# Attention stage of a two-layer trunk: queries' low part on GpSimd, scales in PSUM, two key tiles rounded by ScalarE

## The chip, the cores and the metric

The kernel is one program on one core of a Trainium2 chip. The metric is the device time of one execution in microseconds (us); for the kernel before, it is the median of three runs. A core has five engines that run side by side and wait for each other through semaphores: TensorE (PE, with its weight loads shown apart as PEld), VectorE (DVE), ScalarE (ACT), GpSimd (POOL) and SyncE (SP), which issues most DMAs. Each works through its own instructions in order.

## The reference, cut to what matters

The kernel computes a trunk of two layers, a state-space mixer and then attention, each followed by a feed-forward block, for 1024 latent tokens and 256 context tokens. The change lies in the attention of the second layer. There, queries and keys have 96 features in each of 16 heads, values have 64, and every latent query reads all 1280 keys:

```python
MLA_H = 16
MLA_QK = MLA_NOPE + MLA_ROPE        # 96

def softmax_attend(q, k, v):
    s = jnp.einsum('bqhd,bkhd->bhqk', q, k).astype(jnp.float32) * (MLA_QK ** -0.5)
    p = jax.nn.softmax(s, axis=-1)
    return jnp.einsum('bhqk,bkhd->bqhd', p.astype(v.dtype), v)

def mla_mixer(hx, hc, ...):
    ...
    k_all = jnp.concatenate([kc, kx], axis=1)
    v_all = jnp.concatenate([vc, vx], axis=1)
    ...
    ob = lax.map(lambda qq: softmax_attend(qq, k_all, v_all), qb)
```

Inputs, weights and result are float32.

## The kernel before, in words

TensorE multiplies rounded float32 (`F32R`). To keep precision, an operand is split into a high part, the value rounded, and a low part, the value minus its high part; a product of two split operands then is three matmuls (low by high, high by low, high by high). `split_in` does this for a tile that a DMA has put into its low half: ScalarE writes the rounded copy (`copy`), and an engine that the caller names subtracts (`sub`). All instructions are recorded by one helper line (198), so the profile tells them apart by the names of their tiles.

The attention stage works through 32 units, each one head and one half of the queries (512 of 1024). For a unit it does this:

- Scores. For each of four blocks of 128 queries, `scores_a` multiplies by the first 1024 keys into `psS` (two buffers of two PSUM banks), and VectorE takes the row maximum. `scores_b` multiplies by the last 256 keys into `psE` (one buffer, half of a 2 KB bank), takes their maximum, and one VectorE instruction on single columns takes the larger of the two and multiplies it by the negative scale of the query (`nsc`, an SBUF tile of 128 columns, one for each block and head). ScalarE then writes the exponentials to `p`, from `psE` first and from `psS` second, with the row sums.
- Key tiles. For each of ten tiles of 128 keys, `key_tile` transposes the four blocks of `p` on TensorE into `psT` (two buffers) and makes a high part `ph` and a low part `pl`. Tiles 1, 4, 6 and 9 (`DIRECT`) are rounded by ScalarE from PSUM, and VectorE subtracts, reading PSUM. The six others are copied to SBUF by ScalarE (`pf`), rounded from there by VectorE (the profile's CAST) and subtracted by GpSimd.
- Products. `pv` multiplies `ph` and `pl` by the values (high and low side by side in one weight) into `psO`, one buffer, five tiles (`LAG`) behind the transposes. The last product of a unit is divided by the row sums on VectorE (`rb<-psO,rb`) and stored.

While the ten tiles of a unit are processed, the scores of the next unit are computed between them, at tiles 0, 2, 4 and 6, and the following operands are loaded and split: the queries of the unit after next (`split_q`, at tile 5: ScalarE rounds, VectorE subtracts), the keys of the next head (`split_k`, at tiles 3 and 8 of a head's first half, subtracted by GpSimd) and its values (`split_v`, at tile 3 of the second half, rounded by VectorE and subtracted by GpSimd). Every second head, one feature tile of the output projection's operand is put together (`oa`, `ha`) by GpSimd and ScalarE.

This order is the one in which the program is written. When it is built, a planner arranges the instructions of each engine anew by its own estimate of when they can start, so that the order in the trace differs from it in places; the stage before pins TensorE's order, this one pins none.

Of the kernel before, what the change touches and what calls it, by code (L numbers as in the profile page):

```python
# [18 lines left out]
F32 = mybir.dt.float32  # L19
# [3 lines left out]
ALU = mybir.AluOpType  # L23
# [160 lines left out]
def trunk(tc, I, out, dbg=None):  # L184
# [20 lines left out]
    V, S, Q, T, D_ = (Engine(*e) for e in zip("VSQTD", (nc.vector, nc.scalar, nc.gpsimd, nc.tensor, nc.sync)))  # L205
# [8 lines left out]
    def sub(o, a, b, e=V):  # L214
        e.tensor_tensor(o, a, b, op=ALU.subtract)
# [4 lines left out]
    def copy(o, a):  # L220
        S.activation(o, a, AF.Copy)
# [10 lines left out]
    def split_in(h, l, e):  # L232

        l32 = l.bitcast(F32)
        copy(h, l32)
        sub(l, l32, h.bitcast(F32), e)
# [3 lines left out]
    def pool(name, bufs=1, side="left", space=None):  # L240
        kw = {} if space is None else {"space": space}
        cm = tc.tile_pool(name=name, bufs=bufs, side=side, reuse_waits="tile", **kw)
        p = cm.__enter__()
        opened.append((p, cm))
        return p
# [15 lines left out]
    pp = None  # L261
# [273 lines left out]
    pp = pool("ps0", 4, space=PSUM)  # L535
# [194 lines left out]
    def w_in_split(xc, f):  # L730
        o = hp.tile([128, 2, 640], F32R, name="h")
        split(o[:, 0], o[:, 1], xc[:, f])
        return o
# [20 lines left out]
    h = []  # L754
# [15 lines left out]
    h = [w_in_split(x, f) for f in range(8)]  # L770
# [414 lines left out]
    h = []  # L1185
# [4 lines left out]
    pp = pool("ps1", 4, space=PSUM)  # L1190
# [184 lines left out]
    pp = pool("ps2", 4, space=PSUM)  # L1375
# [4 lines left out]
    pp = ps3 = pool("ps3", 4, space=PSUM)  # L1380
# [7 lines left out]
    nsc = sc.tile([128, 8, HEADS], F32, name="nsc")  # L1388
# [257 lines left out]
    pp = pool("psq", 4, space=PSUM)  # L1646
# [24 lines left out]
    pp = pool("ps4", 2, space=PSUM)  # L1671
# [8 lines left out]
    def load_kv(hd):  # L1680
        kt = kq.tile([128, 2, TOK], F32R, name="kt")
        dma(kt[:, 1].bitcast(F32), kd[hd])
        vt = kq.tile([128, 10, 128], F32R, name="vt")
        vr = kq.tile([128, 10, 64], F32, name="vr", bufs=1)
        dma(vr, vd[hd])
        kv[hd] = kt, vt, vr
# [11 lines left out]
    qts = {}  # L1698
# [4 lines left out]
        qts[n] = qt  # L1703

    def split_q(n):
        split_in(qts[n][:, 0], qts[n][:, 1], V)

    open_s = []

    def scores_a(n, b):  # L1710

        hd, hf = units[n]
        kt, qt = kv[hd][0], qts[n]
        pa = pp.tile([128, 2, 512], F32, name="psS", tag="psS", bufs=2)
        qs = slice(b * 128, b * 128 + 128)
        for j, (qp_, kp_) in enumerate(((1, 0), (0, 1), (0, 0))):
            for o, c0 in ((pa[:, 0], 0), (pa[:, 1], 512)):
                T.matmul(o, qt[:, qp_, qs], kt[:, kp_, c0:c0 + 512], start=j == 0, stop=j == 2)
        flat = pa.rearrange("p a b -> p (a b)")
        mx = at.tile([128, 3], F32, name="mx", bufs=4)  # L1720
        V.reduce_max(mx[:, 0:1], flat, axis=AX.X)
        open_s.append((n, b, flat, mx))

    def scores_b():

        n, b, flat, mx = open_s.pop()
        hd, hf = units[n]
        kt, qt = kv[hd][0], qts[n]
        i = 4 * hf + b
        pb = pp.tile([128, 256], F32, name="psE", tag="psE", bufs=1)  # L1730
        qs = slice(b * 128, b * 128 + 128)
        for j, (qp_, kp_) in enumerate(((1, 0), (0, 1), (0, 0))):
            T.matmul(pb, qt[:, qp_, qs], kt[:, kp_, 1024:], start=j == 0, stop=j == 2)
        V.reduce_max(mx[:, 1:2], pb, axis=AX.X)
        V.scalar_tensor_tensor(mx[:, 2:3], mx[:, 0:1], mx[:, 1:2], nsc[:, i, hd:hd + 1], op0=ALU.max, op1=ALU.mult)
        sc = scq[:, i, hd:hd + 1]
        p = at.tile([128, TOK], F32, name="p", bufs=8)
        S.activation(p[:, 1024:], pb, AF.Exp, bias=mx[:, 2:3], scale=sc, accum_out=rs2[:, hd, hf, 1, b:b + 1])
        S.activation(p[:, :1024], flat, AF.Exp, bias=mx[:, 2:3], scale=sc, accum_out=rs2[:, hd, hf, 0, b:b + 1])
        return p  # L1740

    def key_tile(ps, k):
        tp = pp.tile([128, 512], F32, name="psT", tag="psT", bufs=2)
        for b in range(4):
            T.transpose(tp[:, b * 128:b * 128 + 128], ps[b][:, k * 128:k * 128 + 128], ident)
        ph_ = at.tile([128, 512], F32R, name="ph", bufs=6)
        pl_ = at.tile([128, 512], F32R, name="pl", bufs=6)
        if k in DIRECT:
            copy(ph_, tp)
            sub(pl_, tp, ph_.bitcast(F32))  # L1750
        else:
            pf = at.tile([128, 512], F32, name="pf", bufs=3)
            copy(pf, tp)
            V.tensor_copy(ph_, pf)
            sub(pl_, pf, ph_.bitcast(F32), Q)
        return ph_, pl_

# [41 lines left out]
    LAG = 5  # L1799
    SCORES_AT = (0, 2, 4, 6)  # L1800
    DIRECT = (1, 4, 6, 9)
    ot0 = []
    load_kv(0)
    load_q(0)
    load_q(1)
    split_k(0, 0)
    split_k(0, 1)
    split_q(0)
    split_v(0)
    split_q(1)  # L1810
    cur = []
    for b in range(4):
        scores_a(0, b)
        cur.append(scores_b())
    row_sums(0)
    pend = []
    for n in range(NU):
        hd, hf = units[n]
        nxt = []
        for k in range(10):  # L1820
            if n + 1 < NU and k in SCORES_AT:
                scores_a(n + 1, SCORES_AT.index(k))
            if k == 1 and n + 2 < NU:
                load_q(n + 2)
            if k == 1 and hf == 0 and hd + 1 < HEADS:
                load_kv(hd + 1)
            if k in (3, 8) and hf == 0 and hd + 1 < HEADS:
                split_k(hd + 1, k // 8)
            if k == 3 and hf == 1 and hd + 1 < HEADS:
                split_v(hd + 1)  # L1830
            if k == 5 and n + 2 < NU:
                split_q(n + 2)
            if k == 5 and n % 4 == 1 and n > 4:
                ot0.append(tA1())
                heads_in(at, n // 4 - 1, 0, ot0[-1])
            pend.append((n, k, key_tile(cur, k)))
            if open_s:
                nxt.append(scores_b())
            if k == 9 and n + 1 < NU:
                row_sums(n + 1)  # L1840
            if len(pend) > LAG:
                pv(*pend.pop(0))
        cur = nxt
# [7 lines left out]
    pp = pool("ps5", 8, space=PSUM)  # L1851
# [32 lines left out]
    h, h1, ot1 = [], [], []  # L1884
# [40 lines left out]
```

## Time and profile before

| | |
|---|---|
| median of three runs | 3385.07 us (3384.84 to 3391.26) |
| the profiled execution | 3382.86 us |
| its span in the trace | 3381.1 us |
| PE busy over the span | 94% |
| PEld | 86% |
| DVE | 81% |
| ACT | 52% |
| POOL | 30% |
| attention's first scores and last product | 1963.8 us and 2574.7 us from the span's start |

Busy means that an instruction was under way; matmuls overlap, and their ends are modelled. The shares are over all stages. An instruction's row in a timeline has its start in us from the span's start, its duration in us, the engine, and out<-in by tile names; in brackets stands how long its engine had been idle before it, and what ended that. A row with x3 stands for three instructions in succession.

### The profile page before, as it was taken

To read this page: it belongs to the slowest core of one execution; us is meant where nothing else is said; L and a number is where in the kernel's file an instruction comes from. 1 tells how busy PE (TensorE), PEld (TensorE's weight loads), DVE (VectorE), ACT (ScalarE), POOL (GpSimd) and SP (SyncE) were. 2 spreads that over 40 slices of the span, in tenths; PEclk is the share of its full clock that TensorE was granted. 3 is DMA by queue.
4 is the path that set the end of the run, shared out by engine and by line. 5 is a ranking of instruction groups with operands and counts; after the bars stand their busy time and mean duration, and the time that the engine had idled before them with its cause. 6 is when DMAs were issued, how large, how long until landed. Compare 5 with 4: busy or idle time off the path is not lost. (4 is left out here: it accounts for less than half of the span.)

```text
span 3381.1 us, 55277 instructions
## 1 busy us (share of the span) xinstructions
PE 3176.1 (94%) x20468; PEld 2912.5 (86%) x20468; DVE 2737.1 (81%) x4640; ACT 1746.9 (52%) x3234; POOL 1027.6 (30%) x812
## 2 busy tenths in 40 slices
PE   5898889999999999999999988999899899999999
PEld 3888789999999999999988766777777799889998
DVE  5969967877888898878767678888885788898887
ACT  4467743334333453334555467777774544454443
POOL 2346600102103121121234345555554411221111
PEclk7999999999999999999999999999999999999999
DMA  6468866442232323322426632222216322333332
GB/s 233 131 145 190 172 210 238 165 150 91 100 123 100 110 85 119 101 87 88 133 95 186 191 113 83 71 77 74 82 60 188 109 101 101 101 114 107 103 104 76
DMA packets 191774, 414.67 MB, mean 123 GB/s; under 512 B 22224, under 2 KB 73360, under 8 KB 190480
## 3 DMA queue, kind: packets, MB, share of 16 engines
q1 hardware_dynamic: 182288, 392.27, 36.1%
q0 software_dynamic: 9216, 18.88, 3.2%
q8 instruction: 161, 2.64, 0.3%
q14 instruction: 109, 0.89, 0.1%
HBM read 326.89 MB, written 53.49 MB: 113 GB/s over the span
## 5 line engine op out<-in xcount | busy, mean ns | idle before, releaser
L198 PE MATMUL psB<-hs,wb 128*128 128x320 f32 (+1 forms) x7392 | 1003.0, 298 | 22.7 <-DVE wb L198 15.3
L198 PEld LDWEIGHTS psB<-hs,wb 128*128 128x128 f32 x7392 | 993.1, 190 | 31.3 <-DVE wb L198 19.3
L198 ACT ACTIVATE wb<-wr 128x512 fp32r<-128x512 f32 (+3 forms) x704 | 404.5, 593 | 446.4 <-PE psB L198 219.5
L198 DVE TENSOR_TENSOR wb<-wr,wb 128x512 fp32r<-128x512 f32 (+3 forms) x704 | 491.0, 708 | 163.1 <-ACT wb L198 161.9
L198 PE MATMUL psB<-hb,wb 128*128 128x320 f32 (+1 forms) x3360 | 602.8, 341 | 10.7 <-ACT hb L198 5.4
L198 PEld LDWEIGHTS psB<-hb,wb 128*128 128x128 f32 x3360 | 546.3, 189 | 63.0 <-ACT hb L198 6.7
L198 POOL TENSOR_TENSOR ws<-wr 128x512 f32<-128x512 f32 x176 | 243.6, 1389 | 1150.9 <-DMA wr<-in_fi 533.6
L198 ACT ACTIVATE wb<-ws 128x512 fp32r<-128x512 f32 x352 | 219.2, 627 | 270.7 <-PE psB L198 198.2
L198 POOL TENSOR_TENSOR pl<-pf,ph 128x512 fp32r<-128x512 f32 x192 | 250.5, 1305 | 261.7 <-DVE ph L198 256.2
L198 DVE TENSOR_TENSOR wb<-ws,wb 128x512 fp32r<-128x512 f32 x352 | 274.5, 784 | 29.8 <-ACT wb L198 28.1
L198 PE MATMUL psA<-ha,wb 128*128 128x320 f32 x1680 | 249.9, 311 | 4.4 <-ACT ha L198 4.4
L198 PEld LDWEIGHTS psA<-ha,wb 128*128 128x128 f32 x1680 | 248.9, 189 | 5.0 <-ACT ha L198 4.6
L198 PE MATMUL psS<-kt,qt 128*128 128x512 f32 x768 | 213.2, 403 | 1.3 <-ACT p L198 1.3
L198 PEld LDWEIGHTS psT<-ident,p 128*128 128x128 f32 x1280 | 147.6, 140 | 72.4 <-issue 20.2
L198 PE MATMUL psT<-ident,p 128*128 128x128 f32 x1280 | 189.9, 275 | 20.3 <-DVE pl L198 17.3
L198 DVE TENSOR_REDUCE mx<-psS 128x1 f32<-128x1024 f32 x128 | 155.6, 1215 | 19.6 <-PE psS L198 19.0
L198 PEld LDWEIGHTS psS<-kt,qt 128*128 128x128 f32 x768 | 140.2, 190 | 29.1 <-ACT p L198 2.3
L198 POOL TENSOR_TENSOR acc<-acc,sq 128x640 f32<-128x640 f32 (+1 forms) x51 | 82.8, 1624 | 240.5 <-ACT sq L198 227.5
L198 ACT ACTIVATE p<-psS,mx,scq 128x1024 f32<-128x1024 f32 x128 | 153.9, 1202 | 0.0
L198 ACT ACTIVATE hb<-sg 128x640 fp32r<-128x640 f32 (+1 forms) x104 | 72.1, 693 | 147.5 <-DVE sg L198 147.2
L198 PE MATMUL psO<-ph,vt 128*128 128x512 f32 x320 | 139.7, 437 | 2.4 <-DVE ph L198 0.4
L198 PE MATMUL psA<-h,wb 128*128 128x320 f32 x768 | 119.1, 317 | 20.5 <-ACT h L198 15.2
(340 smaller groups left out, 5464.2 us busy)
## 6 DMA issues: line engine op xcount, KB each, us to landing
wr<-in_fi SPq DMA_DIRECT2D x176, 512.0 KB
wr<-in_mt SPq DMA_DIRECT2D x80, 512.0 KB
wr<-in_swg SPq DMA_DIRECT2D x32, 512.0 KB
wr<-in_fo SPq DMA_DIRECT2D x64, 256.0 KB
wr<-in_fo SPq DMA_DIRECT2D x32, 384.0 KB
ww<-pq POOLq DMA_DIRECT2D x32, 320.0 KB, 5.0
kdr<-big SPq DMA_DIRECT2D x32, 320.0 KB
kt<-kdr SPq DMA_DIRECT2D x16, 640.0 KB
```

Source lines behind the costliest of these rows:

```text
L198: r = f(*a, **k)
```

## The change

The change has three parts, all in the attention stage.

- The subtraction of `split_q` goes from VectorE (`V`) to GpSimd (`Q`).
- The PSUM tile `psE` is taken once, as a whole bank of 512 columns. Its first 256 columns hold the scores of the last keys, as before. The scales `nsc` are copied once into 128 columns of the other half, and the instruction on single columns reads them from there.
- For tiles 3 and 8 of the six copied ones (`TWICE`), ScalarE instead of VectorE rounds `pf` to `ph`. The low part stays with GpSimd.

```diff
     def split_q(n):
-        split_in(qts[n][:, 0], qts[n][:, 1], V)
+        split_in(qts[n][:, 0], qts[n][:, 1], Q)
 
     open_s = []
+    pe = pp.tile([128, 512], F32, name="psE", bufs=1)
+    nscale = pe[:, 256:384].rearrange("p (i h) -> p i h", i=8)
+    V.tensor_copy(nscale, nsc)
...
         i = 4 * hf + b
-        pb = pp.tile([128, 256], F32, name="psE", tag="psE", bufs=1)
+        pb = pe[:, 0:256]
...
-        V.scalar_tensor_tensor(mx[:, 2:3], mx[:, 0:1], mx[:, 1:2], nsc[:, i, hd:hd + 1], op0=ALU.max, op1=ALU.mult)
+        V.scalar_tensor_tensor(mx[:, 2:3], mx[:, 0:1], mx[:, 1:2], nscale[:, i, hd:hd + 1], op0=ALU.max,
+                               op1=ALU.mult)
...
             copy(pf, tp)
-            V.tensor_copy(ph_, pf)
+            if k in TWICE:
+                copy(ph_, pf)
+            else:
+                V.tensor_copy(ph_, pf)
             sub(pl_, pf, ph_.bitcast(F32), Q)
...
     DIRECT = (1, 4, 6, 9)
+    TWICE = (3, 8)
```

## Rows read from the trace of the kernel before

**Rows 1.** Timeline of DVE: first and last unit's product of the stretch.

```profile
2048.43 0.68 DVE L198 TENSOR_TENSOR rb<-psO,rb 128x512 f32<-128x512 f32 x1
...
2500.98 0.68 DVE L198 TENSOR_TENSOR rb<-psO,rb 128x512 f32<-128x512 f32 x1
```

**Rows 2.** Busy time by stretch: length, PE, PEld, DVE, ACT, POOL, clock, DMA, GB/s.

```profile
2048.43:2500.98 452.55, 408.73 (x2330) 323.00 (x2329) 383.44 (x661) 329.54 (x678) 262.47 (x193) 1.00 0.23 76
```

**Rows 3.** Timeline of PE in one period: waits before instructions.

```profile
2218.88 0.63 PE L198 MATMUL psE<-kt,qt 128*128 128x256 f32 x3 [1.05 <-ACT p L198]
...
2226.91 0.63 PE L198 MATMUL psT<-ident,p 128*128 128x128 f32 x4 [1.06 <-DVE pl L198]
...
2231.55 0.62 PE L198 MATMUL psE<-kt,qt 128*128 128x256 f32 x3 [0.76 <-ACT p L198]
...
2256.20 0.62 PE L198 MATMUL psE<-kt,qt 128*128 128x256 f32 x3 [1.21 <-ACT p L198]
```

**Rows 4.** Timelines of POOL, DVE and ACT ahead of the wait at 2218.88.

```profile
2216.57 1.54 POOL L198 TENSOR_TENSOR vt<-vr,vt 128x640 fp32r<-128x640 f32 x1
...
2216.95 1.18 DVE L198 SCALAR_TENSOR_TENSOR mx<-mx,nsc 128x1 f32<-128x1 f32 x1
...
2218.17 0.56 ACT L198 ACTIVATE p<-psE,mx,scq 128x256 f32<-128x256 f32 x1 [1.79 <-DVE mx L198]
```

**Rows 5.** Timelines of POOL and DVE ahead of the wait at 2226.91.

```profile
2224.32 1.29 POOL L198 TENSOR_TENSOR pl<-pf,ph 128x512 fp32r<-128x512 f32 x1 [1.20 <-DVE ph L198]
...
2224.36 1.79 DVE L198 TENSOR_TENSOR qt<-qt 128x512 fp32r<-128x512 f32 x1
2226.08 0.68 DVE L198 TENSOR_TENSOR pl<-psT,ph 128x512 fp32r<-128x512 f32 x1
```

**Rows 6.** Timelines of POOL and DVE ahead of the wait at 2231.55.

```profile
2225.57 3.52 POOL L198 TENSOR_TENSOR kt<-kt 128x640 fp32r<-128x640 f32 x2
...
2227.81 1.56 DVE L198 CAST ph<-pf 128x512 fp32r<-128x512 f32 x1
...
2230.22 0.59 DVE L198 SCALAR_TENSOR_TENSOR mx<-mx,nsc 128x1 f32<-128x1 f32 x1
```

**Rows 7.** Timelines of ACT, and PE once, around copies of tiles 3 and 8.

```profile
2208.14 0.63 ACT L198 ACTIVATE ha<-oa 128x512 fp32r<-128x512 f32 x1 [2.10 <-POOL oa L198]
...
2213.01 0.60 ACT L198 ACTIVATE pf<-psT 128x512 f32<-128x512 f32 x1 [1.04 <-PE psT L198]
2213.57 0.56 ACT L198 ACTIVATE p<-psE,mx,scq 128x256 f32<-128x256 f32 x1
...
2214.49 0.60 PE L198 MATMUL psE<-kt,qt 128*128 128x256 f32 x3
...
2223.19 0.59 ACT L198 ACTIVATE pf<-psT 128x512 f32<-128x512 f32 x1
...
2224.19 0.60 ACT L198 ACTIVATE ph<-psT 128x512 fp32r<-128x512 f32 x1
...
2236.32 0.60 ACT L198 ACTIVATE pf<-psT 128x512 f32<-128x512 f32 x1 [0.43 <-PE psT L198]
```

**Rows 8.** By tile: duration ns min/median/max, first and last start, forms.

```profile
L198 DVE SCALAR_TENSOR_TENSOR mx<-mx,nsc x128: 198/219/1183, 1971.9 to 2557.5; 128x1 f32<-128x1 f32 x128
...
L198 DVE TENSOR_TENSOR qt<-qt x32: 660/871/1803, 1814.4 to 2526.3; 128x512 fp32r<-128x512 f32 x32
...
L198 DVE CAST ph<-pf x192: 397/423/1570, 1986.2 to 2571.9; 128x512 fp32r<-128x512 f32 x192
...
L198 ACT ACTIVATE qt<-qt x32: 621/632/636, 1811.2 to 2525.4; 128x512 fp32r<-128x512 f32 x32
...
L198 DVE SCALAR_TENSOR_TENSOR kt<-dmask,dk,psB x16: 215/218/230, 174.2 to 426.4; 128x16 f32<-128x16 f32 x16
```

**Rows 9.** Timelines of POOL and DVE in the first layer.

```profile
208.85 1.41 POOL L198 TENSOR_TENSOR su<-bpi,bb 128x512 f32<-128x512 f32 x1
...
208.97 0.23 DVE L198 SCALAR_TENSOR_TENSOR kt<-dmask,dk,psB 128x16 f32<-128x16 f32 x1
```

## The prediction

> **What bounds the kernel now.** I read the page first, but its busy shares mix all stages, and the change touches the attention stage alone; so that stage is taken by itself. The last product of each unit (a head and half of the queries) dates the stage: from the one at 2048.43 to the one at 2500.98 there are 24 units [rows 1], so 18.86 us each, or 75.42 for four units (two heads), after which the pattern repeats. In that stretch PE is busy 408.73 of 452.55 us, VectorE (DVE) 383.44, ScalarE (ACT) 329.54 and GpSimd (POOL) 262.47, at full granted clock [rows 2]. PE is nearest to full and still loses some 10%, and the stage is bound by short waits of PE on a chain through DVE and ACT.
>
> Next comes PE's timeline over one period. It shows the waits, and three kinds carry nearly all. A: the last 256 keys' scores (psE, one buffer) wait 1.05 and 1.21 us for ACT's exponential of the block before. B: a transpose (psT) waits 1.06 us for DVE's low part of a tile. C: psE waits 0.76 us for ACT again. B and C come back in the other half of the period at the same length [rows 3]. Each has its cause on DVE, and each time the DVE instruction is stretched by a GpSimd one that runs beside it:
> - A [rows 4]: the one-column maximum-and-scale takes 1.18 us, begun while POOL runs its 1.54 us on vt, and ends when that does. ACT has stood idle 1.79 us for it.
> - B [rows 5]: the queries' low part takes 1.79 us on DVE, begun beside POOL's pl of 1.29, and the low part that frees psT is queued behind it.
> - C [rows 6]: a cast of 1.56 us behind POOL's pair on kt (3.52), then the same maximum-and-scale at 0.59, stand ahead of the exponential.
>
> The views by tile say which DVE instructions stretch [rows 8]. Those with two SBUF tensors do: maximum-and-scale 198 to 1183 ns, queries' low part 660 to 1803. So does the cast from SBUF to SBUF, 397 to 1570. An instruction of the same operation as the maximum-and-scale, with one tensor in SBUF, one in PSUM and a scalar column in SBUF, doesn't: the small one on dmask and psB takes 215 to 230 in all 16 cases. One of these began while POOL was in 1.41 us of work between SBUF tensors, and took 0.23 [rows 9].
>
> **The change part by part.** All prices are per period of four units, in the profiled execution, which took 3382.86 us (span 3381.1 and 1.76 around it), 2 us under the median of the three runs; I subtract from the median.
>
> *Scales in PSUM.* The maximum-and-scale takes mx as first tensor, another column of mx as scalar, and the scales as second tensor. With these in PSUM it has the form of the unstretched small one, so I price it at 0.22 us (median 218) [rows 8]. At A this takes 1.18 - 0.22 = 0.96 us off the chain, less than either wait, and ACT was idle before it: 2 x 0.96 = 1.92. Bounds: 0, if the form stretches all the same, and the 2.26 of the two waits. The new copy of 128x128 runs once; I put it at 0.3 us at most, from the small one's 0.22, and leave it out.
>
> The page "PSUM — Partial Sum Buffer" of the Trainium skill, section "PSUM bank collisions raise a hardware error", has it that two engines must be kept off one bank at the same time, other columns or not. Scales and scores now share a bank, so by that rule PE's next psE would have to wait for the maximum-and-scale; no run here shows such a collision. The order psE, maximum, maximum-and-scale, exponential, next psE already is a chain in this code, so that sum would be the same.
>
> *Queries' low part on GpSimd.* One instruction per unit leaves DVE, 0.66 to 1.80 us [rows 8], and comes to POOL at POOL's price for the same shape, 1.29 [rows 5]. At B the low part that frees psT could start when ACT's copy has ended, at 2224.19 + 0.60 = 2224.79 instead of 2226.08 [rows 5, 7]: 1.29 earlier, more than the wait. B gives 2 x 1.06 = 2.12 (bounds 0 and 2.12). On POOL the new instruction waits for ACT's copy of the queries, and behind it are queued the two kt low parts and the next pl. POOL goes from 262.47/24 = 10.9 to 12.2 us of about 18 per unit. A pl that is 1.3 us late has five key tiles (LAG), about 9 us, before PE wants it, and kt is for the next head: nothing.
>
> *Tiles 3 and 8 on ScalarE.* Two casts per unit leave DVE. ACT's copies, counted in the order 0 to 9, show that tile 3 of a head's second half is the one that meets POOL's pl of tile 2; the 1.56 us cast at C is a tile 0 and stays. With the queries' part gone ahead of it, and a shorter maximum-and-scale (0.59 to 0.22), C's chain comes at least 1.29 + 0.37 us sooner, so its wait goes: 2 x 0.76 = 1.52 (bounds 0 and 1.52).
>
> ACT takes on 8 copies from SBUF to SBUF, 0.63 us each by its copy of the queries (median 632 ns) [rows 8]: 8 x 0.63 = 5.04. Each stands in ACT's queue right behind the tile's first copy, so what follows there comes 0.63 later until ACT's next idle moment [rows 7]. I follow the four places of two units:
> - tile 3 (2213.01): next is the exponential that frees psE, ending at 2214.13; PE began the next psE at 2214.49, 0.36 later. Exposed 0.63 - 0.36 = 0.27.
> - tile 8 (2223.19): the copy of tile 9 would end at 2225.42, so its low part comes 0.66 earlier than now instead of 1.29; of B's 1.06 that leaves 0.66. Exposed 0.40.
> - tile 3 of the other unit: ACT stands idle 0.43 before the copy at 2236.32. Exposed 0.63 - 0.43 = 0.20.
> - tile 8 of the other unit: ACT then stands idle 2.10 before 2208.14. Exposed 0.
>
> That is 0.87 per two units, 1.74 per period; bounds 0 (ACT is idle 452.55 - 329.54 = 123 us of the six periods, 20.5 in each) and all 5.04. The order of the instructions on each engine is worked out anew when the program is built, which no row shows; the bounds stand for that too.
>
> *Sum.* 1.92 + 2.12 + 1.52 - 1.74 = 3.82 us per period. A, B and C need a next head, so they come 15 times each, which is 7.5 periods: 29 us. Forecast 3385 - 29 = 3356 us, 0.85% faster.
>
> **The rivals.**
> - *All hidden.* ACT's idle time swallows every copy: 5.56 x 7.5 = 42 us, 3343. For it: 20.5 us of idle time against 5.04 of work. Against: that idle time shrinks with A and C, whose waits it is.
> - *ScalarE eats it.* Every copy exposed: 0.52 x 7.5 = 4 us, 3381, no difference. For it: pf to ph to exponential is one queue, and psT has two buffers, psE one. Against: the places with 0.43 and 2.10 us of idle time.
> - *Slower: ScalarE becomes the bound.* If the copies are exposed and the exponential at C is then held by ACT's queue and not by DVE, C gives nothing: 1.92 + 2.12 - 5.04 = -1.0, times 7.5 is 7.5 us lost, 3393. It decides from the point where over 80% of the copies' time (4.04 of 5.04) is exposed. The four places above come to 35%.
> - *The scales don't do it.* If the maximum-and-scale is stretched by its scalar column, not by its second tensor, A stays: 1.90 x 7.5 = 14 us, 3371. Against: the 0.23 us beside a busy POOL, with a scalar column in SBUF [rows 9].
> - *The stall only moves.* POOL holds DVE off while it runs; one more POOL instruction of 1.29 us per unit meets the casts that stay, and B's gain goes there: 1.70 x 7.5 = 13 us, 3372. The Trainium skill says so in "Perfetto Trace Analysis", section "Optimizing Scalar/DVE Operations": the two engines share a port, so moving work between them might not help. Against: only tile 0's casts meet long POOL rows now, and they free no PSUM buffer.
>
> **How the numbers follow.** Chances: forecast 0.45, all hidden 0.19, ScalarE eats it 0.12, slower 0.12, the stall moves 0.07, scales 0.05. Measurement tells about 0.2%, 7 us, from nothing. Faster 0.45 + 0.19 + 0.07 + 0.05 = 0.76; same 0.12; slower 0.12. The range goes from somewhat past "all hidden", 6.8 per period with the small waits on ACT's tile copies gone too, 51 us and 3334, up to 3381, where ScalarE eats it; that leaves out the slower case and the ends of the others.
>
> **What would show it.** Right: the period falls from 75.4 to about 71.6; maximum-and-scale at 0.22 us at most everywhere; no queries' low part on DVE and one of 1.3 us on POOL; A and B gone from PE's waits; new small PE waits on ACT. Wrong: long maximum-and-scale instructions remain, or PE's waits on ACT's tile copies and exponentials grow to 5 us per period, or the casts of tiles 0, 2, 5 and 7 lengthen by as much as tiles 3 and 8 saved.

## The result, and the profile after

The changed kernel takes 3344.68 us (median of four runs, 3343.04 to 3347.81), beside 3386.43 us for the kernel before in the same runs: a ratio of 0.9872, 95% interval 0.9857 to 0.9888. That is 42 us or 1.3% faster. The forecast was 29 us and 3356; the range held the time, the size was too small by a third, and the experiments show that two of the four terms of the sum were wrong.

First the stage as a whole. Busy time by stretch in the changed kernel, for the same 24 units as [rows 2] (columns: length; PE, PEld, DVE, ACT, POOL; clock; DMA share; GB/s):

```profile
2043.89:2460.19 416.30, 401.07 (x2327) 323.82 (x2327) 313.91 (x590) 354.83 (x726) 290.44 (x217) 1.00 0.24 82
```

Six periods now take 416.30 us instead of 452.55, so a period went from 75.42 to 69.38. VectorE does 70 us less, ScalarE 25 and GpSimd 28 more, and TensorE is busy for 96% instead of 90%. What TensorE waited for in the six periods, before and then after (waiter, what ended the wait: us in total, times, longest):

```profile
PE psE L198 <- ACT p L198: 22.6, 24, 1.2
PE psT L198 <- DVE pl L198: 15.0, 18, 1.1
PE psT L198 <- ACT pf L198: 3.2, 15, 0.2
```

```profile
PE psO L198 <- DVE rb L198: 7.6, 11, 0.7
PE psE L198 <- ACT p L198: 4.9, 8, 0.9
```

The waits on psE (A and C, [rows 3]) fell from 22.6 to 4.9 us, the ones on psT (B among them) are gone, and a small one on psO is new. Forty us of waits became twelve. That is 28 of the 36 us; the other 8 are TensorE's busy time, 408.73 to 401.07: its matmuls last as long as before and overlap more. The views by tile of the changed kernel (duration in ns, min/median/max), beside [rows 8]:

```profile
L198 DVE SCALAR_TENSOR_TENSOR mx<-mx,psE x128: 200/206/218, 1972.7 to 2513.5; 128x1 f32<-128x1 f32 x128
L198 POOL TENSOR_TENSOR qt<-qt x32: 1281/1291/1468, 1812.1 to 2484.0; 128x512 fp32r<-128x512 f32 x32
L198 DVE CAST ph<-pf x128: 415/429/1807, 1987.7 to 2526.0; 128x512 fp32r<-128x512 f32 x128
L198 ACT ACTIVATE ph<-pf x64: 621/632/646, 1990.9 to 2527.6; 128x512 fp32r<-128x512 f32 x64
```

No maximum-and-scale is stretched any more: 218 ns at most, where the longest had been 1183. The queries' part and the copies on ScalarE have the prices that the prediction took for them. The casts that stay still stretch.

A little of the gain is given back behind the stage. Busy time from the last unit's product to the end, before and after:

```profile
2574.70:3381.00 806.30, 782.14 (x5140) 719.16 (x5138) 658.42 (x1098) 370.98 (x669) 179.38 (x128) 0.99 0.34 111
```

```profile
2530.70:3342.00 811.30, 785.51 (x5140) 721.67 (x5138) 659.99 (x1098) 371.79 (x669) 178.94 (x128) 0.98 0.34 111
```

The same instructions take 5 us longer, at a granted clock lower by 0.01. The other kernels of this study show 808 to 817 us there. That is one profiled execution of each; why was not tested.

### The profile page after: what moved, and what is told of

Same layout as the page of the kernel before. It is cut to its first block, busy times and chain, and to the rows that moved or that the text cites. A ratio compares the mean times of both kernels' runs of the same rounds, so it can differ in the third digit from the quotient of the medians.

```text
span 3342.1 us, 55323 instructions
## 1 busy us (share of the span) xinstructions
PE 3169.2 (95%) x20468; PEld 2912.5 (87%) x20468; DVE 2652.4 (79%) x4545; ACT 1781.5 (53%) x3298; POOL 1064.9 (32%) x844
## 5 line engine op out<-in xcount | busy, mean ns | idle before, releaser
L198 PEld LDWEIGHTS psT<-ident,p 128*128 128x128 f32 x1280 | 154.9, 140 | 49.0 <-ACT pf L198 15.7
```

Of the source, the lines that this page charges most:

```text
L198: r = f(*a, **k)
```

## The experiments

The change has three parts, so the first six kernels are all the other ways to have or not have them. The period is that of four units in the profiled execution, from 24 units as above. Each ratio is to runs of the kernel before that were made beside the kernel named, whose medians were 3385.03 to 3388.25 us; a difference between two medians can be off by as much. The profiled execution need not lie at the median: for scales and queries it was the slowest of ten (3391.45 us), and for scales only of four (3370.29 us).

| kernel | median us | ratio to before | 95% interval | period us |
|---|---|---|---|---|
| before | 3386.43 | 1 | | 75.42 |
| scales only | 3361.26 | 0.9930 | 0.9910 to 0.9951 | 71.86 |
| queries only | 3385.17 | 1.0004 | 0.9993 to 1.0016 | 75.23 |
| tiles only | 3369.92 | 0.9954 | 0.9940 to 0.9968 | 72.83 |
| scales and queries | 3382.44 | 0.9987 | 0.9975 to 0.9999 | 75.68 |
| queries and tiles | 3358.81 | 0.9925 | 0.9908 to 0.9942 | 71.36 |
| scales and tiles | 3342.85 | 0.9870 | 0.9852 to 0.9888 | 69.26 |
| all three (the change) | 3344.68 | 0.9872 | 0.9857 to 0.9888 | 69.38 |

The table already says that the queries' part does nothing by itself and nothing on top of the other two. On top of the scales alone it takes most of their gain away again (some 20 us), and on top of the tiles alone it gives 11 (3369.92 to 3358.81).

**Scales only.**

```diff
+    pe = pp.tile([128, 512], F32, name="psE", bufs=1)
+    nscale = pe[:, 256:384].rearrange("p (i h) -> p i h", i=8)
+    V.tensor_copy(nscale, nsc)
...
-        ... mx[:, 1:2], nsc[:, i, hd:hd + 1], ...
+        ... mx[:, 1:2], nscale[:, i, hd:hd + 1], ...
```

> Only the scales go to PSUM; queries and key tiles as in the kernel before. The order of every engine is that of the kernel before but for the one added copy. Theory (the stretched maximum-and-scale is what wait A stands on): no maximum-and-scale over 0.25 us, wait A gone, 1.92 us per period, 14 us faster, about 3372. Rival (the gain of the whole change comes from the new order of instructions): the order is unchanged here, so within 4 us of 3386. Rival (the scalar column stretches it): maximum-and-scale still up to 1.2 us, no change.

Measured: 24 us faster, more than the 14 of wait A. TensorE's waits over its six periods (431.13 us from 2049.64):

```profile
PE psT L198 <- DVE pl L198: 16.2, 23, 1.1
PE psT L198 <- ACT pf L198: 4.6, 14, 0.4
PE psE L198 <- ACT p L198: 4.4, 14, 0.4
```

The waits on psE fall from 22.6 to 4.4 us with nothing else changed, and B's on psT stay. That is 3.0 per period or 23 us for 7.5 periods: the measured gain. It is A as a whole and half of C, whose maximum-and-scale went from 0.59 to about 0.2. In this kernel the programs run in the order of the kernel before on every engine, but for the one copy and TensorE's first block of scores, so the gain is the stretch alone.

**Queries and tiles, without the scales.** The whole change with the `nsc` lines as before.

> The whole change without the scales in PSUM. The order of every engine is that of the changed kernel but for the one copy. Theory: maximum-and-scale is stretched again up to 1.2 us beside GpSimd, and the scales' share of 14 us is given back: about 3358. Rival (with TensorE nearly full, DVE's stalls are covered in the new order): within 4 us of 3345.

Measured: 3358.81, so 14 us are given back, as the theory said. The maximum-and-scale stretches again:

```profile
L198 DVE SCALAR_TENSOR_TENSOR mx<-mx,nsc x128: 206/219/1176, 1972.4 to 2528.1; 128x1 f32<-128x1 f32 x128
```

**Queries only.**

```diff
     def split_q(n):
-        split_in(qts[n][:, 0], qts[n][:, 1], V)
+        split_in(qts[n][:, 0], qts[n][:, 1], Q)
```

> Only the queries' low part goes to GpSimd. Theory: waits B and most of C go, 2.12 to 3.64 us per period, 16 to 27 us faster, 3359 to 3370. Rival (GpSimd and VectorE share the port, so the stall only moves to the casts): casts lengthen by about what the queries' part took, and the time is within 7 us of 3386.

Measured: no difference, though VectorE is busy 21 us less in six periods and B's wait is gone. The casts lengthened from 630 to 661 ns in the mean, 4.5 us in all for 144 of them, which is too little for the rival's reason. TensorE's waits show a longer one in its place, and new ones behind small VectorE work on the row sums' reciprocals (`r`, `rt`):

```profile
PE psE L198 <- ACT p L198: 33.8, 24, 2.9
PE psT L198 <- DVE rt L198: 8.0, 11, 0.8
PE psT L198 <- DVE r L198: 1.3, 1, 1.3
```

The 2.9 us come once a period. The timelines of GpSimd, ScalarE and TensorE around one of them:

```profile
2130.53 1.30 POOL L198 TENSOR_TENSOR qt<-qt 128x512 fp32r<-128x512 f32 x1
...
2131.79 1.46 POOL L198 TENSOR_TENSOR oa<-oa,ob 128x512 f32<-128x512 f32 x1
...
2133.28 0.63 ACT L198 ACTIVATE ha<-oa 128x512 fp32r<-128x512 f32 x1 [3.35 <-POOL oa L198]
...
2135.35 0.56 ACT L198 ACTIVATE p<-psE,mx,scq 128x256 f32<-128x256 f32 x1 [0.95 <-DVE mx L198]
...
2136.06 0.62 PE L198 MATMUL psE<-kt,qt 128*128 128x256 f32 x3 [2.92 <-ACT p L198]
```

Every second head GpSimd adds the halves of a head pair (`oa`) and ScalarE rounds the sum (`ha`). The queries' part now stands ahead of `oa` on GpSimd. ScalarE, which works in order, stands 3.35 us in front of `ha<-oa`, with the exponential that frees psE queued behind it. Beside it ScalarE waits for GpSimd in a second way, since `pf` has three buffers and GpSimd's low part frees them:

```profile
ACT pf L198 <- POOL pl L198: 10.7, 22, 0.6
```

**Queries only, with oa on VectorE.** This tests that reading: the queue ahead of `ha` is shortened, the rest left.

```diff
-        add(oa, oa, ob, Q)
+        add(oa, oa, ob, V if p is at else Q)
```

> The queries' part alone on GpSimd, as before, and the sum of the two head halves (oa) in the attention stage on VectorE instead of GpSimd. Theory (what eats the gain is ScalarE's copy of ha, which stands ahead of the exponentials and waits for oa, which stands on GpSimd behind the queries' part): the 2.9 us wait of TensorE once per period goes; 15 to 20 us faster than the queries' part alone, 3365 to 3370. Rival (the gain is lost to casts stretched by GpSimd): unchanged, 3380 to 3388.

Measured: 3369.32, ratio 0.9944 (0.9930 to 0.9959), so 16 to 19 us faster than the queries' part alone, as expected. No run has `oa` on VectorE with the queries' part left there too, so how much of this is the shorter way to `ha` by itself isn't known. TensorE's waits on psE are back to at most 1.1 us:

```profile
PE psE L198 <- ACT p L198: 18.6, 24, 1.1
PE psT L198 <- DVE rt L198: 8.8, 12, 0.7
PE psT L198 <- DVE pl L198: 3.5, 6, 0.6
```

**Scales and queries, without the tiles.** The whole change with `V.tensor_copy(ph_, pf)` for all six copied tiles.

> Scales and queries' part, without the two tiles on ScalarE. The prediction's steps: all of 5.56 us per period and no copies on ScalarE, 42 us faster, 3343, as fast as the whole change or a little faster. Rival (parts add up as they were measured alone): 24 us for the scales and 0 for the queries, 3361, so the tiles on ScalarE are worth 16 us of the whole change instead of costing 13.

Measured: 3382.44, worse than both expectations. The prediction's steps would have made this the best kernel. Its TensorE stands at the same place as with the queries' part alone:

```profile
2139.31 1.01 PE L198 MATMUL psE<-kt,qt 128*128 128x256 f32 x3 [2.91 <-ACT p L198]
```

Here the wait costs more than itself. The three matmuls behind it take 1.01 us where they took 0.62: from 2139.3 to 2143.8 the granted clock was 0.62, so for part of that time TensorE ran at the lower of its two levels, 1.2 of 2.4 GHz. The clock fell so behind each of these waits in the stretch. With the queries' part alone it stayed at 1.00 behind all but one of the waits of the same length, and why it differs is open. Over 23 units (the row that follows) TensorE was busy 17.29 us per unit:

```profile
2049.59:2485.53 435.94, 397.74 (x2232) 320.64 (x2231) 339.90 (x612) 318.49 (x649) 280.31 (x206) 0.97 0.23 75
```

**The same with oa on VectorE.**

> Scales and queries' part without the tiles, and the sum oa in the attention stage on VectorE. Theory (the queries' part on GpSimd costs through the queue oa, ha, exponential): the 2.9 us wait per period goes, at least 20 us faster than the same kernel with oa on GpSimd (3382), so at or under 3362, which scales alone gave. Rival (in the order that the queries' part brings, other waits hold TensorE anyway): 3375 to 3385.

Measured: 3363.26, ratio 0.9925 (0.9905 to 0.9944), one us short of what was expected. The 2.9 us wait is gone and with it some 20 us, which brings the kernel to where the scales alone are. Its busy time and TensorE's waits, over 24 units:

```profile
2042.45:2474.44 431.99, 404.95 (x2330) 324.95 (x2328) 358.75 (x643) 332.57 (x678) 289.95 (x210) 1.00 0.24 79
...
PE psE L198 <- ACT p L198: 8.5, 24, 0.8
PE psT L198 <- DVE rt L198: 8.0, 11, 0.7
PE psO L198 <- DVE rb L198: 5.8, 12, 0.5
```

TensorE is busy 16.87 us per unit at full clock. Of the 22 us by which six periods are shorter (454.1 to 432.0), some 10 are thus the clock and some 12 the waits. And even without the long wait the queries' part adds nothing to the scales: the casts take 102.6 us, beside 90.8 with the scales alone, and the waits behind `rt` and `rb` are new.

**Tiles only.**

```diff
-            V.tensor_copy(ph_, pf)
+            if k in TWICE:
+                copy(ph_, pf)
+            else:
+                V.tensor_copy(ph_, pf)
...
+    TWICE = (3, 8)
```

> Only tiles 3 and 8 are rounded by ScalarE. By the prediction's step the eight copies are exposed for 1.74 us per period: 13 us slower, 3399, unless casts taken off VectorE give something back. Theory formed on the result (ScalarE's idle time hides the copies, and the stretched casts of tile 3 gone are a gain that the prediction left out): faster by 0 to 10 us, 3376 to 3386.

Measured: 15 us faster, against 13 us slower by the prediction's step. TensorE's waits over its six periods (436.95 us):

```profile
PE psE L198 <- ACT p L198: 21.9, 18, 1.4
PE psT L198 <- DVE pl L198: 4.9, 12, 0.4
```

It is B that goes, from 15.0 to 4.9 us, while the waits on psE stay as a sum (21.9, in 18 waits instead of 24). The timelines of VectorE, ScalarE and GpSimd at B's place, to be held against [rows 5], show how:

```profile
2106.41 0.63 ACT L198 ACTIVATE ph<-pf 128x512 fp32r<-128x512 f32 x1
2106.84 0.67 DVE L198 TENSOR_TENSOR qt<-qt 128x512 fp32r<-128x512 f32 x1
2107.12 1.55 POOL L198 TENSOR_TENSOR pl<-pf,ph 128x512 fp32r<-128x512 f32 x1 [1.17 <-ACT ph L198]
```

Tile 8 is rounded by ScalarE behind the queries, so GpSimd's pl of that tile starts 0.28 us after the queries' low part on VectorE and not 0.04 before it. Now VectorE takes its 0.67 and GpSimd is the one that is held (1.55 instead of 1.29). Over the 24 units the queries' part on VectorE took 800 ns in the mean, where it had been 1279.

**Scales and tiles, without the queries' part.** The whole change with `V` in `split_q`.

> The whole change without the queries' part, which stays on VectorE. The prediction's step: wait B comes back, 2.12 us per period, 16 us given back, about 3361. Rival (after the queries' part alone gave nothing): scales alone gave 24 us and tiles alone 15, which add up to 39, so 3346, and the queries' part is worth nothing here either.

Measured: 3342.85, the same as the whole change. The gains of scales (24) and tiles (15) add up to 39, the whole gain but for a few us.

**Copies on ScalarE doubled.** The whole change, and each of the two copies done twice.

```diff
             if k in TWICE:
                 copy(ph_, pf)
+                copy(ph_, pf)
```

> The whole change with each of the two rounding copies on ScalarE done twice, 5.04 us more of ScalarE per period. If ScalarE's idle time hides the copies: within 5 us of 3345. If copies on ScalarE are exposed in full: 5.04 x 7.5 = 38 us slower, 3383. The prediction's share of 35%: 13 us slower, 3358.

Measured: 3340.75, ratio 0.9858 (0.9843 to 0.9873), no slower than the change itself with 4.4 us more of ScalarE's busy time per period. Busy time over its six periods:

```profile
2040.00:2451.32 411.32, 402.68 (x2330) 324.29 (x2329) 333.14 (x589) 381.08 (x775) 291.58 (x216) 1.00 0.25 83
```

ScalarE is busy for 381 of 411 us, 93%, and the six periods are 5 us shorter than with the copies done once. Its added work is not on TensorE's path in the order that this kernel gets; ScalarE, VectorE and GpSimd run in another order here than in the change, so the test isn't of the copies alone. The rows of the change itself say the same. After each of the 48 copies of its six periods ScalarE stands idle for 0.28 us or more before the next exponential that frees psE, so no copy held that up. One of them:

```profile
2198.19 0.63 ACT L198 ACTIVATE ph<-pf 128x512 fp32r<-128x512 f32 x1
...
2200.37 0.57 ACT L198 ACTIVATE p<-psE,mx,scq 128x256 f32<-128x256 f32 x1 [0.56 <-DVE mx L198]
```

**Tiles 0 and 5 instead of 3 and 8.** The whole change with `TWICE = (0, 5)`.

> The whole change with tiles 0 and 5 instead of 3 and 8 rounded by ScalarE. The same work on each engine. Theory (what counts is that VectorE does two casts less, and TensorE is nearly full): within 7 us of 3345. Rival (it counts which tiles: tile 8's later low part lets the queries' part and oa through, tile 3's cast is one of those that stretch): 10 us or more above 3345.

Measured: 3378.53, ratio 0.9975 (0.9963 to 0.9988): the choice of tiles is worth 34 us. ScalarE's waits in its six periods:

```profile
ACT qt L198 <- DMA qt<-qd: 20.6, 12, 2.6
ACT ha L198 <- POOL oa L198: 18.9, 6, 3.2
ACT kt L198 <- DMA kt<-kdr: 12.8, 10, 1.5
```

In the order that this kernel gets, ScalarE stands in front of transfers and of `oa` again, for 52 us in six periods. In the changed kernel the same three come to 0, 6.0 and 0.8. Some of the time is the clock again, 0.98 over the six periods, where TensorE was busy 409.54 us instead of 401.07. The placement and the load changed together here, so what belongs to which tile is not told apart.

**Tiles 0, 3 and 8.** The whole change with `TWICE = (0, 3, 8)`.

> The whole change with tile 0 rounded by ScalarE as well, whose cast still stretches to 1.8 us. Theory (ScalarE has room left, as the doubled copies showed): 0 to 6 us faster than the whole change, 3338 to 3345; TensorE at 96% allows little more. Rival (three copies a unit are too many): above 3350.

Measured: 3323.09 us, ratio 0.9806 (0.9784 to 0.9828), better than the theory allowed and the fastest kernel of the study, 22 us under the change. Its profiled execution took 3336.19, above that median; in it the period is 67.23 us. ScalarE's waits for `oa` and for transfers don't appear at all, and TensorE waits 6.5 us in six periods:

```profile
PE psE L198 <- ACT p L198: 3.3, 12, 0.3
PE psO L198 <- DVE rb L198: 3.2, 6, 0.7
```

**The change with oa on VectorE.**

> The whole change with the sum oa in the attention stage on VectorE. Theory: ScalarE's wait for oa is 1 us per period there, which the changed kernel already covers for the most part; 0 to 6 us faster, 3338 to 3345. Rival (VectorE's extra 0.7 us per period and stretch cost as much): within 2 us of 3345 or above.

Measured: 3351.97, ratio 0.9890 (0.9870 to 0.9910), no gain: 7 us above the change, as the second expectation had it. The period is 69.46 us, as in the change; there is no long wait for `oa` to remove.

## Why the prediction was right or wrong, point by point

*The number: in part luck.* The four terms were 14 (scales), 16 (queries) and 11 (C) less 13 (tiles), 29 us; measured alone, the scales gave 24, the queries 0 and the tiles 15, 39 us. Errors of both signs kept the time in the range.

*What bounds the stage: right.* TensorE's waits on psE and psT behind stretched VectorE instructions were the loss. They came to 6.8 us per period and fell to 2.1; with the 1.3 us less of TensorE's busy time that makes the 6.0 us by which the period got shorter.

*Scales in PSUM: the mechanism right, the term too small.* The form with one tensor in PSUM isn't stretched, as the small instruction of the first layer had shown [rows 8, 9]. The term was 1.92 us per period, 14 us. Alone the scales gave 24 us, as they also took half of C, which the prediction had booked jointly with the queries' part. Taken out of the whole change they cost the 14.

*Queries' low part on GpSimd: wrong.* The term was 2.12 us per period, 16 us; it measured 0 alone and 0 within the change, some 20 lost on top of the scales and 11 gained on top of the tiles. The step that failed is the sentence that the added GpSimd work costs nothing, because TensorE wants pl five tiles later. It followed only one reader of GpSimd's queue. Two others are ScalarE's, `ha<-oa` and the three buffers of `pf`, and ScalarE's queue holds the exponential that frees psE. With this part alone, 18.2 us of waits on psT went in six periods; 11.2 us came back on psE, through the new wait of 2.9, and 9.3 on psT behind VectorE's small copies. The kernels with `oa` on VectorE show the first; the second stays in them and was not tested. The rival "the stall only moves" gave the right time for this part, but the casts took only 4.5 of the 21 us that VectorE was freed of. With the scales in, where the casts took 12 us more, it can't be ruled out as a part of the reason. The Trainium skill's sentence in "Perfetto Trace Analysis", section "Optimizing Scalar/DVE Operations", that moving work between these two engines might not help, came out right for this part alone; the runs put much of the reason in the order of the queues.

*Tiles 3 and 8 on ScalarE: wrong in sign.* The term was a cost of 1.74 us per period, 13 us; alone the tiles gave 15 us, and no copy of the changed kernel held up the exponential that frees psE. The four places were followed in the order of the trace of before, but the programs are put in order anew, and there ScalarE stood idle between each copy and that exponential. What the step left out is that the change of engine also moves GpSimd's pl of tile 8 behind the queries' part. With the tiles alone that is where B went, for which the prediction had relied on the queries' part; the order of all engines changed with it, so this is read from the rows and not tested by itself.

*C: half shown.* Half of it went with the scales. Which part took the other half was not separated.

*The rivals.* "All hidden" (3343) came nearest to the measured 3344.68, and its statement on the copies is shown. Its sum still held the queries' 16 us, which weren't there, and lacked the tiles' gain, so that it came so near is luck. Slower, "ScalarE eats it" and "the scales don't do it" are out by ScalarE's idle time behind each copy and by the 218 ns.

*Still open.* The 5 us given back behind the stage, and how much of the tiles' 38 us within the change (3382 to 3345) is the order that the planner gives and how much the clock, which was lower in the kernel without them.

## What to carry to other kernels

When an instruction is moved to an idle engine, follow every reader of that engine's queue, buffers that it frees included, up to the engine that bounds the stage; a share of busy time says little, as ScalarE at 93% cost nothing while 1.3 us on a GpSimd that was 58% busy cost a wait of 2.9. Where two engines hold each other off, it can be enough to change which of them starts first, or to put one operand in PSUM. Where a planner orders the instructions, measure each part alone and each left out: the queries' part was worth nothing, a loss of some 20 us or a gain of 11, by what else was there.

## What the runs showed of the hardware

- In the rows above the hold works both ways and by who starts first: with 0.28 us of lead VectorE's 128x512 subtraction took 0.67 us and GpSimd's 1.55; with GpSimd 0.04 ahead, VectorE's took 1.79 and GpSimd's 1.29.
- Scales and scores in one PSUM bank cost nothing that can be seen: the maximum-and-scale took 194 to 219 ns in every one of the 128 cases with the scales alone, and no wait on it grew.
- The same wait of TensorE of 2.9 us was followed by full clock in one kernel (three matmuls in 0.62 us, clock 1.00 in the 4.5 us behind it) and by a lower one in another (1.01 us, 0.62).
